# Strassen's scheme for the output projection of layer 0, with its products grouped by form

## The chip, the cores and the metric

One core of a Trainium2 chip runs the whole kernel in one launch. The metric is device microseconds (us) of that core. TensorE (PE) multiplies, VectorE (DVE) and ScalarE (ACT) do the elementwise work, GpSimd (POOL) and SyncE (SP) mostly issue transfers; each engine works through its instructions in order.

## What is computed

A trunk of two residual layers over 528 positions (16 meta tokens and a sequence of 512), model width 2048. Cut to what matters here:

```python
for layer in range(DEPTH):                       # DEPTH = 2
    hn = rms_norm(h, norm_gain[layer])
    y = even_mixer(hn, ...) if layer % 2 == 0 else odd_mixer(hn, ...)
    h = h + y
# the end of even_mixer (layer 0):
return jnp.concatenate([a_out, b_out], axis=-1) @ w_out      # (528 x 2048) @ (2048 x 2048)
# the end of odd_mixer (layer 1):
return o @ w_out                                             # (512 x 2048) @ (2048 x 2048)
```

`a_out` (1024 channels) comes from a convolution branch, `b_out` (1024 channels) from eight sparse attention heads.

## The kernel before, in words

Everything lies transposed: channels on the 128 partitions, positions along the free dimension (T = 528, cut in two halves of HT = 264). A vector of 2048 channels is 16 tiles of 128x528. The weights lie in DRAM in stripes of 128 output channels; a stripe is two halves of 128x1024 fp32 (512 KB), each with eight 128x128 blocks for 1024 input channels.

Matrix products are made in three passes: weights and inputs are split into a high and a low part, and `products` (L170 to L178) issues hi by hi, hi by lo and lo by hi for each of 8 blocks, so 24 matmuls for one weight half and one half of the positions. `load_half` (L140 to L148) loads a weight half on SP's queue into one of 2 staging tiles `w32`, copies it to `wh` on ACT (L146) and subtracts for `wl` on DVE (L147); `wh` and `wl` have 3 buffers each. `stripe` (L150) uses one weight half for both halves of the positions: 2 x 2 x 24 = 96 matmuls a stripe. `split` (L187 to L192) does the same splitting for an input tile.

Layer 0 runs in the order of the list `EVEN`: convolution (`glu`), index scores (`scores`), top-k selection (`select`), eight heads (`head`, with `attend`), then eight gate stripes that finish the tiles `MA[0..7]` of `a_out` (L608 to L620). `attend` writes each head's result to DRAM (`mbd`, L561). In `attend`, for each block of 128 queries, POOL issues a transfer of the bias rows (L516), then one that adds the mask in flight (L518); DVE takes both up at L526. The tiles `L` that they fill have 3 buffers.

**The stage that is changed** (L624 to L659): the eight `mbd` tiles are loaded and split, then the eight `MA` tiles; then 16 stripes, each with the `mbd` half first (`order=(1, 0)`). For each output tile the residual input is loaded on SP's queue (L645), DVE adds the two PSUM parts (L649), the sum is split for layer 1 (L190, L191), written to DRAM as `h1d` on SP's queue (L651), and squared and accumulated for the next norm (L656, L657).

**Layer 1** runs 16 recurrent heads, each with three stripes, while POOL's queue makes sums of weight halves in DRAM (`weight_sums`, L861 to L878: copies, and additions in flight). Then come 16 gate stripes, and then its own output projection, which already uses Strassen's scheme: the 2x2 blocks of weights and inputs give 7 products in place of 8, 56 products of 24 matmuls of 256 columns, each with a weight half of its own; every third load has a third staging tile, `w33`.

The order on each engine is set at build time by a scheduler that simulates the kernel; `band(level)` gives a stretch of code its priority (`WGT` 5 for weights, `EVAC` 4, `SIDE` 3, `CONV` 2). Among what is ready by that simulation, the higher band goes first.

Of the kernel before, what the change touches and what calls it, by code (L numbers as in the profile page):

```python
# [18 lines left out]
SEQ = 512  # L19
# [53 lines left out]
def trunk_kernel(ctx: ExitStack, tc: tile.TileContext, x: bass.AP, w: bass.AP, wukv: bass.AP,  # L73
# [42 lines left out]
    ones_c = ones_of(1.0 / 256, "ones_c")  # L116
    ones_a = ones_of(1.0 / 1024, "ones_a")
    ones_h = cst([128, 128], F32R, "ones_h")
    S.activation(ones_h, ones_c, AF.Copy, scale=2.0)
# [3 lines left out]
    V.memset(c15, 1.5)  # L123
    eps_l = cst([128, 1], F32, "eps_l")
# [3 lines left out]
    for _ in range(10):  # L128
        P.matmul(warm[:, :128], ones_d, ones_a, start=True, stop=True)
# [9 lines left out]

    def load_half(src, pool=wpool, names=("wh", "wl"), bufs=3, m=128, w32=None):  # L140
        w32 = w32 or wpool.tile([128, 1024], F32, name="w32", bufs=2)
        Q.dma_start(w32, src)
# [27 lines left out]
    def products(o, hi, lo, X, start, stop, m=128):  # L170

        issued = []
        for k, (xh, xl) in enumerate(X):
# [3 lines left out]
            issued.append(P.matmul(o, lo[:, ws], xh, start=False, stop=stop and k == 7))  # L177
        return issued  # L178

    def evac(dst, parts, rstd):  # L180
        o = T - dst.shape[-1]
        for p, sl in parts:
            V.tensor_tensor(dst[:, sl.start - o:sl.stop - o], p[:dst.shape[0]], rstd[:dst.shape[0], sl],  # L183
                            op=OP.mult)

# [20 lines left out]
    def rstd_from(pieces, dst, eps, tmp=None):  # L206

        for p, sl in pieces:
            S.activation(dst[:, sl], p, AF.Ln, bias=eps)
            S.activation(dst[:, sl], dst[:, sl], AF.Exp, scale=-0.5)  # L210
            if tmp is not None:
                t = tmp[:, sl]
                S.activation(t, dst[:, sl], AF.Square)
                V.scalar_tensor_tensor(t, p, eps, t, op0=OP.add, op1=OP.mult)
                S.activation(t, t, AF.Identity, scale=-0.5, bias=c15)
                V.tensor_tensor(dst[:, sl], dst[:, sl], t, op=OP.mult)

# [5 lines left out]
    r1 = tc.tile_pool(name="r1", bufs=KT, side="left")  # L223
    r1p = r1.__enter__()
    ev = ExitStack()
    epools = {}
# [4 lines left out]
    for role in ("em", "es", "ec", "ek", "ei"):  # L231
        epools[role] = ev.enter_context(tc.tile_pool(name=role, bufs=2, side="right"))
# [152 lines left out]
    with band(SIDE):  # L385
        rc = et([128, T], F32, "acc", 2)
        rstd_from(mean_bcast(ones_c, csq, None), rc, eps_r, et([128, T], F32, "sq", 3))
# [47 lines left out]
    def scores(j):  # L435
        ps = stripe(S_QI + j, X0, wide=False)

# [38 lines left out]
    def glu(i):  # L476
        ps = stripe(S_GLU + 2 * i, X0)
        g = et([128, T], F32, "gt", 3)
# [3 lines left out]
        ps = stripe(S_GLU + 2 * i + 1, X0)  # L482
        v = et([128, T], F32, "gt", 3)
# [94 lines left out]
    def layer_norm():  # L578
        with band(CONV):
# [5 lines left out]
            for p, sl in mean_bcast(ones_a, [zs], None):  # L585
                S.activation(mu[:, sl], p, AF.Copy)
# [10 lines left out]
            rstd_from(mean_bcast(ones_a, [vs_], None), rz, eps_l)  # L597
# [307 lines left out]

# [274 lines left out]
```

## Time and profile before

| | |
|---|---|
| median of 3 runs | 1944.06 us (1943.9 to 1944.37) |
| the profiled execution | 1945.34 us |
| its span, first to last instruction | 1943.1 us |
| mean granted TensorE clock | 0.997 of full |
| HBM read, written | 223.12 MB, 44.78 MB |
| PE / DVE / ACT / POOL busy | 99% / 70% / 44% / 6% |

Busy shares are over the whole span. A matmul's duration in the profile covers its way through the array, and the next one starts long before it ends; the time from one start to the next tells more than the duration. DVE and ACT instructions overlap a little as well. The idle time of an engine stands beside the instruction that followed it, with what ended it. The time of the runs contains some 2 us around the span.

### The profile page before, as it was taken

Reading aid. Unit: us, or ns where it says so; the run is one execution under the profiler, and the core shown is the slowest. Engines: PE = TensorE matmul, PEld = TensorE weight load, DVE = VectorE, ACT = ScalarE, POOL = GpSimd, SP = SyncE. Lnnn points to the kernel's source line nnn. Section 1 sums busy time; section 2 is a strip of 40 time slices with the busy share of each in tenths; the row PEclk is TensorE's granted clock in tenths of the full one; section 3 lists DMA queues with packets and bytes.
Section 4 is the critical chain, followed back from the end, with each engine's and each line's share of the span. In section 5 each row is a group of like instructions: output and inputs, shape, how many; then the busy total and the mean of one; then the engine's idle time right before and its main releaser. Section 6 shows DMA issues by size and latency. Waiting matters only on the chain.

```text
span 1943.1 us, 36429 instructions
## 1 busy us (share of the span) xinstructions
PE 1922.4 (99%) x14998; PEld 1813.8 (93%) x14998; DVE 1357.0 (70%) x2581; ACT 846.7 (44%) x1475; POOL 119.4 (6%) x202
## 2 busy tenths in 40 slices
PE   9999999999999999999999999999999999999997
PEld 8999899999999999999999999999999988889997
DVE  7699989997466444443677777777777775558766
ACT  6332442234435433322554545454555443235554
POOL 1000000111110100000000000000000000000000
PEclk9999999999999999999999999999999999999998
DMA  6323333344342434444644453444445423226665
GB/s 211 106 87 93 102 89 105 92 120 117 105 116 83 122 127 132 136 135 141 158 120 120 131 145 117 131 120 120 140 115 149 120 77 109 92 93 215 187 185 174
DMA packets 77302, 244.59 MB, mean 126 GB/s; under 512 B 9744, under 2 KB 17464, under 8 KB 76624
## 3 DMA queue, kind: packets, MB, share of 16 engines
q1 hardware_dynamic: 62656, 194.21, 30.8%
q0 software_dynamic: 14192, 47.86, 11.2%
q8 instruction: 118, 1.93, 0.4%
q14 instruction: 48, 0.39, 0.1%
q10 hardware_dynamic: 288, 0.19, 0.0%
HBM read 223.12 MB, written 44.78 MB: 138 GB/s over the span
## 4 chain that ended last, share of the span: by engine, by line
PE 80%; DVE 1%; DMA 0%; ACT 0%; issue 0%; DVEq 0%
PE mps L177 22%; PE mps L175 22%; PE mps L176 22%; PE s L176 1%; PE s L177 1%; PE s L175 1%; PE po L549 1%; PE s L524 1%; PE s L718 1%; PE s L717 1%; PE s L719 1%; PE po L840 1%; PE po L839 1%; PE s L836 1%; PE s L420 1%; PE s L407 0%
## 5 line engine op out<-in xcount | busy, mean ns | idle before, releaser
L175 PE MATMUL mps<-xh,wh 128*128 128x264 f32 (+2 forms) x3504 | 1074.2, 307 | 5.1 <-ACT xh L190 2.4
L177 PE MATMUL mps<-xh,wl 128*128 128x264 f32 (+2 forms) x3504 | 1075.1, 307 | 0.0
L176 PE MATMUL mps<-xl,wh 128*128 128x264 f32 (+2 forms) x3504 | 1073.7, 307 | 0.1
L175 PEld LDWEIGHTS mps<-xh,wh 128*128 128x128 f32 x3504 | 660.6, 189 | 34.9 <-ACT xh L190 2.6
L176 PEld LDWEIGHTS mps<-xl,wh 128*128 128x128 f32 x3504 | 659.5, 188 | 30.5 <-issue 0.6
L177 PEld LDWEIGHTS mps<-xh,wl 128*128 128x128 f32 x3504 | 659.7, 188 | 27.3
L146 ACT ACTIVATE wh<-w 128x1024 fp32r<-128x1024 f32 x313 | 331.5, 1059 | 595.1 <-PE mps L176 487.8
L147 DVE TENSOR_TENSOR wl<-w,wh 128x1024 fp32r<-128x1024 f32 x313 | 382.9, 1223 | 200.5 <-ACT wh L146 194.9
L494 DVE SCALAR_TENSOR_TENSOR z<-u,vec,z 128x528 f32<-128x528 f32 x240 | 180.6, 763 | 2.6
L183 DVE TENSOR_TENSOR gt<-mps,rstd 128x264 f32<-128x264 f32 (+1 forms) x80 | 38.5, 482 | 74.5 <-PE mps L177 73.5
L713 ACT ACTIVATE qhm<-q 128x256 f16<-128x256 f32 x128 | 51.8, 417 | 56.4 <-DVE q L815 44.3
L176 PE MATMUL s<-xl,wh 128*128 128x256 f32 (+1 forms) x240 | 67.7, 282 | 0.0
L175 PE MATMUL s<-xh,wh 128*128 128x256 f32 (+1 forms) x240 | 67.5, 281 | 0.0
L177 PE MATMUL s<-xh,wl 128*128 128x256 f32 (+1 forms) x240 | 67.4, 281 | 0.0
L800 DVE COPY_PREDICATED A<-msk,s 128x256 f32<-128x256 uint8 x96 | 46.5, 485 | 28.4 <-PE s L719 27.8
L714 DVE SCALAR_TENSOR_TENSOR qlm<-q,qhm 128x256 f16<-128x256 f32 x128 | 53.0, 424 | 15.8 <-ACT qhm L713 15.7
L649 DVE TENSOR_TENSOR hin<-mps,hin 128x264 f32<-128x264 f32 x32 | 13.8, 433 | 46.4 <-PE mps L177 46.4
L459 ACT ACTIVATE sq<-s 128x264 f32<-128x264 f32 (+3 forms) x80 | 29.2, 393 | 39.0 <-PE s L457 32.3
L713 ACT ACTIVATE kt1h<-k 128x256 f16<-128x256 f32 x64 | 26.5, 414 | 44.5 <-DVE k L806 44.5
L176 PEld LDWEIGHTS s<-xl,wh 128*128 128x128 f32 x240 | 45.1, 188 | 0.6 <-issue 0.6
L175 PEld LDWEIGHTS s<-xh,wh 128*128 128x128 f32 x240 | 45.2, 188 | 0.0
L177 PEld LDWEIGHTS s<-xh,wl 128*128 128x128 f32 x240 | 45.2, 188 | 0.0
(366 smaller groups left out, 2521.3 us busy)
## 6 DMA issues: line engine op xcount, KB each, us to landing
w<-in_w_dram SPq DMA_DIRECT2D x283, 512.0 KB, 3.7
ws<-in_w_dram POOLq DMA_DIRECT2D x48, 512.0 KB, 6.0
w<-ws SPq DMA_DIRECT2D x32, 512.0 KB, 3.6
ws<-ws POOLq DMA_DIRECT2D x16, 512.0 KB, 5.0
hin<-in_x_dram SPq DMA_DIRECT2D x16, 264.0 KB, 3.7
h1d<-hin SPq DMA_DIRECT2D x16, 264.0 KB, 2.1
on<-h1d SPq DMA_DIRECT2D x14, 256.0 KB, 4.2
z<-in_x_dram SPq DMA_DIRECT2D x8, 264.0 KB, 5.3
```

Source lines behind the costliest of these rows:

```text
L146: S.activation(uh, used, AF.Copy)
L147: V.tensor_tensor(ul, used, uh.bitcast(F32), op=OP.subtract)
L175: P.matmul(o, hi[:, ws], xh, start=start and k == 0, stop=False)
L176: P.matmul(o, hi[:, ws], xl, start=False, stop=False)
L177: issued.append(P.matmul(o, lo[:, ws], xh, start=False, stop=stop and k == 7))
L183: V.tensor_tensor(dst[:, sl.start - o:sl.stop - o], p[:dst.shape[0]], rstd[:dst.shape[0], sl], op=OP.mult)
L420: P.matmul(p[:ns, :256], CX[k][b][:, s0:s0 + ns], a[:, ws], start=n == 0, stop=n == 5)
L459: S.activation(r[:, :s1 - s0], p[:, :s1 - s0], AF.Relu)
L494: eng.scalar_tensor_tensor(z, u[:, j:j + T], col(V_CW + i * CW + j), z, op0=OP.mult, op1=OP.add)
L713: S.activation(hi, src, AF.Copy, scale=scale)
L714: V.scalar_tensor_tensor(lo, src, scale, hi, op0=OP.mult, op1=OP.subtract)
L800: V.copy_predicated(A.rearrange("p b (n a m) -> p b n a m", a=2, m=mm)[:, :, :, 1, :], msk[:, li - 1 + i:li + i, :].rearrange("p b (n m) - ...
```

## The change

The output projection of layer 0 is made of 7 products per pair of output tiles (output tiles p and p+8, for p from 0 to 7), over the two halves of positions and the two halves of input channels. All first products of the eight pairs run, then all of the next form: order 1, 5, 6, 7, 4, 3, 2.

- Weight sums for layer 0 (8 pairs, 8 transfers each, 512 KB each) are made in DRAM during layer 0: 16 plain copies on SP's queue behind weight loads of `scores` and `glu`, 48 copies and additions on POOL's queue behind the mask additions of the softmax. Those of layer 1 go on as before, 4 per recurrent head.
- The seven input forms: B11, N1 and N2 are split into a new pool `xf` in the place of three pools of layer 0; N2 reads `mbd` and writes an intermediate `tfd` to DRAM; T3, T4 (from `tfd`), B22 and B21 (from `mbd`) are loaded again on POOL's queue and split into the tiles `xh`, `xl` of layer 0's input.
- The residual inputs and outputs `C[0..15]` are held in tiles of layer 0 that are done with. Their loads and the writes of `h1d` move from SP's queue to POOL's.
- Layer 1's input `X1` goes into the tiles `xh`, `xl` again, rather than into a pool of its own. The first stripe of layer 1 and its last gate stripe take their halves in the order (1, 0).
- The first three products run seven of their eight blocks each, and the eighth blocks afterwards.
- The third staging tile is used for products 9, 12, 15, ... of both Strassen stages. In layer 1 it was used for every third from the third on.
- Three constants for means become one, with the factor moved into ACT's scale.

```diff
-        P.matmul(warm[:, :128], ones_d, ones_a, start=True, stop=True)
+        P.matmul(warm[:, :128], ones_d, ones_d, start=True, stop=True)
...
+    def sum_step(what, m, pair):
+        a = {11: w[pair[0], 0], 12: w[pair[0], 1], 21: w[pair[1], 0], 22: w[pair[1], 1]}
+        if what == "copy":
+            dst = wsum[pair, m] = dram.tile([128, 1024], F32, name=f"ws{pair[0]}_{m}")
+            src = {7: a[11], 5: a[21], 6: wsum.get((pair, 5)), 3: wsum.get((pair, 6))}[m]
+            return (Q if m in (5, 7) and pair in EPAIRS else G).dma_start(dst, src)
+        src = {7: a[21], 5: a[22], 6: a[11], 3: a[12]}[m]
+        return G.dma_start(wsum[pair, m], src, accum_op=OP.add, max_dma_last_dim=4096)
...
+    def strassen_weights(pair, m, pool, at):
+        own = at > 6 and at % 3 == 0
+        return load_half(product_weights(pair, m),
+                         w32=pool.tile([128, 1024], F32, name="w33", bufs=1) if own else None)
...
     def glu(i):
         ps = stripe(S_GLU + 2 * i, X0)
+        some_steps(plain_steps, 1, loaded[0])
...
-                G.dma_start(e[:, :W], M[t], accum_op=OP.add)
+                masked = G.dma_start(e[:, :W], M[t], accum_op=OP.add)
+                some_steps(steps, 1 + t % 2, masked)
...
-    for n in range(KT):
-        with band(EVAC):
-            hin = U.tile([128, T], F32, name="hin1", bufs=2)
-            Q.dma_start(hin, x[n])
-        ps = stripe(S_OE + n, MX, order=(1, 0))
...
     with band(SIDE):
+        for z in MA:
+            early_form0("B11", z[:, LT])
+        for z in MA:
+            n1 = et([128, T], F32, "sq", 3)[:, LT]
+            V.tensor_tensor(n1, z[:, LT], z[:, RT], op=OP.subtract)
+            early_form0("N1", n1)
+        for i, z in enumerate(MA):
+            mb = et([128, T], F32, "sq", 3)
+            G.dma_start(mb, mbd[i])
+            V.scalar_tensor_tensor(mb[:, RT], mb[:, RT], 2.0, z[:, RT], op0=OP.mult, op1=OP.subtract)
+            V.scalar_tensor_tensor(z[:, LT], mb[:, RT], -1.0, z[:, LT], op0=OP.mult, op1=OP.subtract)
+            V.scalar_tensor_tensor(mb[:, LT], mb[:, LT], -2.0, z[:, LT], op0=OP.mult, op1=OP.subtract)
+            G.dma_start(tfd[i], mb)
+            early_form0("N2", z[:, LT])
+        for name, src, sl, scale in (("T3", tfd, RT, 0.25), ("T4", tfd, LT, 0.25), ("B22", mbd, RT, 0.5),
+                                     ("B21", mbd, LT, 0.5)):
+            for j in range(0, 8, 2):
+                both = et([128, T], F32, "sq", 3)
+                G.dma_start(both.rearrange("p (n t) -> p n t", n=2), src[j:j + 2, :, sl].rearrange("n p t -> p n t"))
+                hl = split(r1p, both, scale)
+                forms0[name] += [[t[:, c] for t in hl] for c in (LT, RT)]
...
+    def finish1(n):
+        X1[n] = split(r1p, C[n], col(V_G1 + n))
+        G.dma_start(h1d[n], C[n])
...
+    turns = [(p, m) for m in (1, 5, 6, 7, 4, 3, 2) for p in range(8)]
+    for at, (pr, m) in enumerate(turns):
+        u, c0, c1 = us[pr], C[pr], C[8 + pr]
+        o = (mps if at % 7 < 3 else ps1)()[:, :HT]
+        with band(WGT):
+            hi, lo = strassen_weights(EPAIRS[pr], m, xfp, at)
+        X = forms0[FORM[m]]
+        if at < 3:
+            products(o, hi, lo, X[:7], True, False)
+            held.append((o, hi[:, 896:], lo[:, 896:]))
+            if at < 2:
+                continue
+            for o, hi, lo in held:
+                products(o, hi, lo, X[7:], False, True)
+        else:
+            products(o, hi, lo, X, True, True)
+        with band(EVAC):
+            if m == 1:
...
+                    S.activation(us[p], o, AF.Copy)
+                    V.tensor_tensor(C[p][:, LT], C[p][:, LT], o, op=OP.add)
+            elif m == 5:
+                V.tensor_tensor(c0[:, RT], c0[:, RT], o, op=OP.add)
+                V.tensor_tensor(c1[:, RT], c1[:, RT], o, op=OP.subtract)
+            elif m == 6:
+                V.tensor_tensor(u, u, o, op=OP.add)
+                V.tensor_tensor(c0[:, RT], c0[:, RT], u, op=OP.add)
+            elif m == 7:
+                V.tensor_tensor(u, u, o, op=OP.add)
+                both = c1.rearrange("p (c t) -> p c t", c=2)
+                V.tensor_tensor(both, both, u[:, None, :].to_broadcast([128, 2, HT]), op=OP.subtract)
+            elif m == 4:
+                V.tensor_tensor(c1[:, LT], c1[:, LT], o, op=OP.subtract)
+                finish1(8 + pr)
+            elif m == 3:
+                V.tensor_tensor(c0[:, RT], c0[:, RT], o, op=OP.add)
...
+                V.tensor_tensor(c0[:, LT], c0[:, LT], o, op=OP.add)
+                last = finish1(pr)
...
-        ps = stripe(S_FQV + 3 * h, X1)
+        ps = stripe(S_FQV + 3 * h, X1, order=(0, 1) if h else (1, 0))
...
-        weight_sums(h // 2, h % 2, cleared)
+        some_steps(osteps, 4, cleared)
```

## Rows read from the trace of the kernel before

**Rows 1.** The page's parts 1 and 2: busy time, the span in 40 slices.

```profile
PE 1922.4 (99%) x14998; PEld 1813.8 (93%) x14998; DVE 1357.0 (70%) x2581; ACT 846.7 (44%) x1475; POOL 119.4 (6%) x202
...
PE   9999999999999999999999999999999999999997
```

**Rows 2.** Evacuations of the changed stage, DVE's timeline: start, us, instruction, idle before.

```profile
762.42 0.43 DVE L649 TENSOR_TENSOR hin<-mps,hin 128x264 f32<-128x264 f32 x1 [0.70 <-PE mps L177]
...
914.96 0.43 DVE L649 TENSOR_TENSOR hin<-mps,hin 128x264 f32<-128x264 f32 x1 [0.70 <-PE mps L177]
917.88 0.43 DVE L649 TENSOR_TENSOR hin<-mps,hin 128x264 f32<-128x264 f32 x1 [2.49 <-PE mps L177]
```

**Rows 3.** The end of the last gate stripe, DVE's timeline.

```profile
727.19 0.43 DVE L183 TENSOR_TENSOR gt<-mps,rstd 128x264 f32<-128x264 f32 x1 [1.20 <-PE mps L177]
...
731.16 0.70 DVE L619 TENSOR_TENSOR z<-z,gb 128x528 f32<-128x528 f32 x1
```

**Rows 4.** The changed stage's first stripe, PE's timeline.

```profile
733.47 0.28 PE L177 MATMUL mps<-xh,wl 128*128 128x264 f32 x1
736.11 0.63 PE L175 MATMUL mps<-xh,wh 128*128 128x264 f32 x3 [2.36 <-ACT xh L190]
```

**Rows 5.** Windows: us, busy time by engine, PEclk, DMA share, GB/s.

```profile
core 0: us, PE busy (x) PEld busy (x) DVE busy (x) ACT busy (x) POOL busy (x), PEclk, DMA share, GB/s
698.00:727.00 29.00, 29.00 (x239) 29.00 (x239) 15.48 (x22) 9.67 (x14) 0.00 (x0) 1.00 0.43 137
727.00:745.00 18.00, 15.53 (x126) 15.11 (x125) 11.76 (x18) 9.18 (x16) 0.00 (x0) 1.00 0.27 81
745.00:915.00 170.00, 170.00 (x1394) 170.00 (x1392) 68.31 (x90) 49.17 (x60) 0.95 (x1) 1.00 0.42 139
1790.00:1920.00 130.00, 130.00 (x1097) 130.00 (x1096) 92.28 (x136) 72.56 (x104) 0.00 (x0) 1.00 0.60 186
925.00:960.00 35.00, 35.00 (x282) 32.81 (x281) 24.97 (x56) 18.34 (x38) 4.52 (x7) 1.00 0.74 181
0.00:20.00 20.00, 17.96 (x117) 15.93 (x118) 14.23 (x33) 15.75 (x27) 3.84 (x16) 1.00 0.94 333
```

**Rows 6.** Groups of instructions of the changed stage (745 to 915 us).

```profile
L147 DVE TENSOR_TENSOR wl<-w,wh 128x1024 fp32r<-128x1024 f32 x30 | 36.8, 1225 | 59.1 <-ACT wh L146 59.1
L146 ACT ACTIVATE wh<-w 128x1024 fp32r<-128x1024 f32 x30 | 31.7, 1058 | 121.9 <-PE mps L176 71.1 <-issue 50.7
...
L191 DVE SCALAR_TENSOR_TENSOR xl<-hin,vec,xh 128x528 fp32r<-128x528 f32 x15 | 11.5, 763 | 0.0
L190 ACT ACTIVATE xh<-hin,vec 128x528 fp32r<-128x528 f32 x15 | 10.8, 720 | 0.0
L657 DVE TENSOR_TENSOR acc<-acc,sq 128x528 f32<-128x528 f32 x14 | 9.8, 702 | 0.0
```

**Rows 7.** A split of 256 columns, and eight back to back (DVE).

```profile
L919 DVE TENSOR_TENSOR xl<-on,xh 128x256 fp32r<-128x256 f32 x32 | 11.6, 419 | 0.0
...
737.37 5.03 DVE L191 SCALAR_TENSOR_TENSOR xl<-z,xh 128x528 fp32r<-128x528 f32 x8
```

**Rows 8.** Weight splits in layer 1's Strassen stage: first and last start.

```profile
L146 ACT ACTIVATE wh<-w x46: 1058/1062/1062, 1789.6 to 1917.5; 128x1024 fp32r<-128x1024 f32 x46
```

**Rows 9.** Transfers, median us from issue to landing: 745 to 915, then 925 to 960.

```profile
w<-in_w_dram SPq DMA_DIRECT2D x30, 512.0 KB, 3.7
...
w<-in_w_dram SPq DMA_DIRECT2D x6, 512.0 KB, 4.2
ws<-in_w_dram POOLq DMA_DIRECT2D x4, 512.0 KB, 7.4
```

**Rows 10.** A head's last query block: mask transfer issued, DVE's use; then all mask transfers.

```profile
638.91 0.87 POOL L518 DMA_DIRECT2D L<-mask  x1 [4.32 <-PE s L546]
...
645.91 0.42 DVE L526 CUSTOM_DVE_ANT_0 L<-s,L 128x264 f32<-128x264 f32 x1
...
DMA to landing us min/median/max: 2.4/3.5/5.8
```

**Rows 11.** Two of the eight lines of weight sums in layer 1, on POOL's queue.

```profile
L871 POOL DMA_DIRECT2D ws<-in_w_dram x8: 514/516/517, 921.1 to 1488.8; - x8
L872 POOL DMA_DIRECT2D ws<-in_w_dram x8: 838/844/849, 925.4 to 1493.8; - x8
```

More of the change, by code (lines that the diff above doesn't have):

```diff
@@ L176, in products @@
             P.matmul(o, hi[:, ws], xl, start=False, stop=False)
-            issued.append(P.matmul(o, lo[:, ws], xh, start=False, stop=stop and k == 7))
+            issued.append(P.matmul(o, lo[:, ws], xh, start=False, stop=stop and k == len(X) - 1))
         return issued
@@ L221, in trunk_kernel @@
     h1d = dram.tile([KT, 128, T], F32, name="h1d")
[L223 to L226, printed above, removed]
+    tfd = dram.tile([8, 128, T], F32, name="tfd")
+    r1p = ctx.enter_context(tc.tile_pool(name="r1", bufs=KT, side="left", reuse_waits="tile"))
+    epools, eopen = {}, {}
     def et(shape, dt, name, bufs):
         return epools[EROLE.get(name, "es")].tile(shape, dt, name=name, bufs=bufs)
-    for role in ("em", "es", "ec", "ek", "ei"):
-        epools[role] = ev.enter_context(tc.tile_pool(name=role, bufs=2, side="right"))
+    for role in ("em", "ec", "es", "ek", "ei"):
+        eopen[role] = tc.tile_pool(name=role, bufs=2, side="right")
+        epools[role] = eopen[role].__enter__()
     E = epools["ek"]
@@ L622, in trunk_kernel @@
         tap("ma7", MA[7])
-    MX = [None] * KT
-    with band(SIDE):
-        for i in range(8):
-            mb = et([128, T], F32, "mb", 2)
-            Q.dma_start(mb, mbd[i])
-            MX[8 + i] = split(r1p, mb, 0.5)
-        for i in range(8):
-            MX[i] = split(r1p, MA[i], 0.25)
-    ev.close()
-    r2 = tc.tile_pool(name="r2", bufs=KT, side="right", reuse_waits="tile")
-    r2p = r2.__enter__()
-    up = tc.tile_pool(name="up", bufs=2, side="right", reuse_waits="tile")
-    U = up.__enter__()
@@ L639, in trunk_kernel @@
[L639 to L659 removed]
+    for role in ("ei", "ek", "es"):
+        eopen[role].__exit__(None, None, None)
@@ new lines, in trunk_kernel, with early_form0 @@
+    keep = ctx.enter_context(tc.tile_pool(name="keep", bufs=1, side="left", reuse_waits="tile"))
+    xf = tc.tile_pool(name="xf", bufs=1, side="right", reuse_waits="tile")
+    xfp = xf.__enter__()
+    LT, RT = slice(0, HT), slice(HT, T)
+    forms0 = {name: [] for name in FORM.values()}
+    def early_form0(name, src):
+        hi, lo = [xfp.tile([128, HT], F32R, name=n, bufs=24) for n in ("fh", "fl")]
+        split2(hi, lo, src, 0.25)
+        forms0[name].append((hi, lo))
+    with band(SIDE):
+        for z in MA:
[19 more added lines that the diff above has]
+                forms0[name] += [[t[:, c] for t in hl] for c in (LT, RT)]
@@ L928, in late_form @@
         if i % 2 == 0:
-            late[name] = [r2p.tile([128, T], F32R, name=n, bufs=KT) for n in ("xh", "xl")]
+            late[name] = [r1p.tile([128, T], F32R, name=n, bufs=KT) for n in ("xh", "xl")]
         sl = slice(i % 2 * HS, (i % 2 + 1) * HS)
@@ L976, in trunk_kernel @@
                 late_form(name, i)
[L979 to L986 removed]
     pending = []
     H2 = [None] * KT
[L989 removed]
+    acc2 = keep.tile([128, T], F32, name="rstd1", bufs=1)[:, :SEQ]
     done = [0, 0]
```

135 lines of the change are left out of this document (73 added, 62 removed).

## The prediction

> **What bounds the kernel now.** I read the page's busy times first, then the windows of the changed stage, then the starts of its evacuations, its waits and its transfers. PE is busy in 1922.4 of 1943.1 us and in nearly every slice [rows 1]: a microsecond leaves the time only if PE has fewer matmuls or fewer gaps. In the stage itself PE is busy in 170.0 of 170 us at full granted clock, DVE in 68.3, ACT in 49.2, POOL in 0.95, and the transfers move 139 GB/s [rows 5]. So the stage lasts as long as its matmuls take to issue. The first evacuation of a stripe comes at 762.42 us, that of the stripe 13 further on at 914.96 [rows 2]: 11.734 us a stripe, 122.2 ns a matmul (96 of them), 2.933 us for the 24 of one product.
>
> **What is removed.** 16 stripes are 64 groups of 24 matmuls; Strassen's scheme leaves 56. Eight groups by 2.933 us are **23.5 us**. The second term is a wait: between the last evacuations of the gate stripes (727.19) and of the stage (917.88) [rows 2, 3] lie 190.7 us, and 16 stripes by 11.734 are 187.7, so some **2.9 us** are lost. They are where PE stood from 733.47 to 736.11 for the split of a late `mbd` tile [rows 4]. The new order doesn't need `mbd` until the third group of products, so this wait goes.
>
> The Trainium skill (TensorE: Matmul & The Clock Gate, section Back-to-back issue gap) gives N/2.4 + 2.5 ns for an isolated gap, 112.5 ns for 264 columns; by it the first term would be 21.6 us. The measured 122.2 ns decides.
>
> **What is added, in the order of the stage.** First the start. B11 needs `MA[7]`, whose last product ends some 4.7 us after the last gate evacuation (731.16 + 0.70 against 727.19) [rows 3], and after that come a copy on ACT and a subtraction on DVE of 264 columns, about 0.4 us each as in the 256-column row [rows 7]. The three products of seven blocks cover 63 matmuls, 7.7 us, so no wait here. But they keep all three pairs of weight buffers until their eighth blocks have run. Only then can the fourth product's weights be split: 1.06 us on ACT, then 1.22 on DVE [rows 6], about 0.2 for the handovers, against six held matmuls (0.7) and two that need no `wl` (0.2): **1.6 us** of wait.
>
> Then the staging tiles. Until product 9 there are only two, and a product now uses up a weight half in 2.933 us where a stripe took 5.87. A staging tile is taken for the landing (3.7 us, 4.2 beside POOL's sums [rows 9]) and the split (2.3): 6.0 to 6.5 us for two products that take 5.87. With the cushion of ready weights used up by the held blocks, I count waits of a few tenths at products 5 and 7 by the 3.7, and about 1 us each by the 4.2. Bounds 0.7 and 4 us (the 7.4 that a landing on POOL's queue took [rows 9] would be the worst case for one or two of them); I take **2 us**, as the stage's start is where its extra loads crowd. From product 9 on three tiles serve three products in 8.8 us, enough up to a landing of about 6 us. Layer 1 has this steady state now: 46 splits from 1789.6 to 1917.5, 2.84 us each [rows 8], with PE busy throughout [rows 5]. Its own third tile now comes in later; there the buffers start full, which I cost at nothing, between nothing and 1 us.
>
> **DVE** gets close to its limit. Per stage: 56 weight subtractions (1.225) 68.6 us; 72 evacuating operations of 264 columns (0.433, [rows 2]) and 8 of 528 (0.70) 36.8; 16 finished tiles (0.763 and 0.702 [rows 6]) 23.4; forms, 56 operations of 264 (0.42 [rows 7]) and 16 of 528 (0.70) 34.7. Together 163.5 us of busy time in 56 x 2.933 = 164.3. Three things relieve it. Instructions back to back overlap: eight of 0.70 took 5.03 us, not 5.6 [rows 7], which is a tenth of it all. The forms of `MA[0..6]` can be made in the 29 us before the stage, where DVE is busy in 15.5 [rows 5]. And weights come first in priority, while seven PSUM buffers let an evacuation be up to six products late. What is left is a load of 80 to 90%, against the 71% (92.3 of 130) that layer 1's stage bears without a wait [rows 5]. Bounds 0 and 8 us (the overdue work of the second group, two evacuations a product plus what remains of N2); I take **2 us** together with what follows.
>
> **Queues and transfers.** SP loses 40 transfers of 264 KB and gets 16 copies behind weight loads in layer 0, where a weight half lasts over 5 us: nothing, 0 to 1 us. POOL, idle in the stage, issues 64 transfers there at 0.5 to 0.85 us [rows 11]. What waits in that queue: a load of `mbd` stands behind a write of `tfd` whose tile it needs, and the loads of `C[8..15]` behind N2. With three such tiles the eight rounds of N2 take some 25 us; due is the last one 47 us after the start, T3's at 70 us. The transfers of the stage are 56 weight halves (29.4 MB), residuals in and out (8.7 MB), `mbd` and `tfd` (8.7 MB): 46.7 MB in 164 us, 285 GB/s. The trace has 186 GB/s at a share of 0.60 and 333 at 0.94 [rows 5], so this is high but below what was reached.
>
> At the **handover** to layer 1, X1[4..7] overwrite the B21 tiles and are split only after the last product: four times 0.72 and 0.763 [rows 6] with a weight split between them, about 5 us. The first stripe begins with the other half, 48 matmuls, 5.9 us. Nothing, 0 to 1 us.
>
> In the **attention**, 48 sums join POOL's queue, 0.5 to 0.85 us each [rows 11]. What is behind them is the next block's bias transfer. The mask of a head's last block is issued at 638.91 and used at 645.91; it takes 0.87 us and 3.5 to land, so about 2.6 us are spare, in the tightest head [rows 10]. One or two sums and a slower landing take about that. I cost it at nothing, 0 to 5 us.
>
> **Sum**, on the profiled execution's 1945.34 us: -23.5 - 2.9 + 1.6 + 2 + 2 = -20.8, so 1924.5. The median of the runs lies 1.3 us below that execution: **1923 us**. No change, as far as a measurement tells, is within 0.2%, 3.9 us.
>
> **Rivals.**
> *Transfers hold the stage.* If the crowded start (loads of C, `mbd`, `tfd`, all beside the weights) or the 285 GB/s can't be kept up, weights land late again and again. At 260 GB/s, halfway between the two rows, 46.7 MB take 180 us, 16 more: 1937. For it: weights landed in 4.2 us rather than 3.7 beside only four sums [rows 9]. Against it: 333 GB/s in the first 20 us [rows 5]. The Trainium skill (DMA: Bandwidth & Descriptors, section Issuing engines are not separate DMA queues) says that transfers from any queue share the same 16 engines and interleave; by that rule moving them to POOL's queue spares the weights nothing, and the two landings in [rows 9] agree. Chance 0.14, 1930 to 1940.
>
> *Slower than before: the masks.* The sums' transfers run beside the softmax's bias and mask transfers. If a mask lands later than the spare 2.6 to 5 us, DVE waits at L526 with the weight subtractions queued behind it, and PE follows once the ready weights are used. There are 8 such last blocks. To cancel the gain, each must lose over 2.6 us, that is a mask 7 us late or more; at 12 us, each loses about 7 and the time is 1923 + 56 = 1979; at 8 us, 1923 + 28 = 1951. For it: a sum took 7.4 us to land [rows 9]. Against it: the mask is 3.5 us at the median and 5.8 at most [rows 10], and the other blocks' masks are issued far ahead. Chance 0.07.
>
> *It doesn't shorten the stage.* If weights arrive at no better than one per 3.35 us, 56 of them take as long as before: 1944. It would take a landing of over 7 us on three tiles. Chance 0.04; layer 1's 2.84 us speaks against it.
>
> *Nothing new waits* but the fourth product: 1944.06 - 26.4 + 1.6 = 1919. The chance of 1917 to 1920 is 0.10.
>
> **The numbers.** My own case, waits of 3 to 10 us in all, 1920 to 1930, has 0.65. With the other cases: faster by over 0.2% 0.88, the same 0.05, slower 0.07. The range 1917 to 1937 holds the better case, my own and most of the first rival.
>
> **What would show it.** Right: 192 matmuls fewer; last gate evacuation to last product of the stage about 170 us, not 190.7; a wait of PE for `wh` or `wl` at the fourth product; DVE busy in over 80% of the stage; weights landing in 4 to 5 us there; attention without new waits of PE. Wrong: PE waits for weights spread over all seven groups (transfers), waits of DVE for DMA at L526 (masks), or at N2 and T3 (forms late).

## The result, and the profile after

The changed kernel takes **1923.73 us** (median of 4 runs, 1923.7 to 1924.42) where the kernel before takes 1943.98 on the same chip (1943.82 to 1944.37): a ratio of 0.9896, 95% interval 0.9879 to 0.9914. The profiled execution took 1923.71 us, its span is 1921.9. Other chips of the study gave the kernel before 1944.8 to 1945.3 and the changed one 1925.72, so times below are set against runs on the same chip.

The page's busy times of the changed kernel, the answer to [rows 1]:

```profile
PE 1897.4 (99%) x14806; PEld 1790.5 (93%) x14806; DVE 1421.1 (74%) x2708; ACT 883.5 (46%) x1531; POOL 193.6 (10%) x314
```

There are 192 matmuls fewer, and PE is still busy nearly all the time. To see where the microseconds went, the span is cut at three places in PE's timeline: the first product of layer 0's output stage, the first matmul of layer 1, and the first product of layer 1's output stage.

| us | until layer 0's output | layer 0's output | layer 1's heads and gates | layer 1's output to the end | span |
|---|---|---|---|---|---|
| before | 726.98 | 190.69 | 850.68 | 174.71 | 1943.1 |
| after | 728.51 | 167.97 | 848.51 | 176.94 | 1921.9 |
| difference | +1.5 | -22.7 | -2.2 | +2.2 | -21.2 |

At the 2.933 us of the kernel before, 56 products take 164.3 us, which leaves 3.7 us of delay. But where no wait falls, this stage's matmuls start a little closer: 121.67 ns apart (1137 starts in a row from 758.01 to 896.36 us) in place of 122.2. That makes 2.920 us a product and 163.5 us for 56, so the delay is 4.4 us. Windows of the changed kernel over the stage (columns as in [rows 5]); the last row is all of it:

```profile
728.72:752.00 23.28, 21.52 (x171) 20.66 (x169) 19.62 (x40) 12.56 (x25) 5.38 (x10) 1.00 0.70 232
752.00:775.00 23.00, 22.01 (x176) 21.57 (x177) 18.57 (x36) 10.41 (x14) 7.06 (x14) 1.00 0.91 312
775.00:799.00 24.00, 24.00 (x199) 24.00 (x198) 22.36 (x40) 13.40 (x16) 7.55 (x12) 1.00 0.94 345
...
728.72:897.60 168.88, 166.13 (x1354) 164.84 (x1353) 142.96 (x227) 95.12 (x129) 33.53 (x57) 1.00 0.77 263
```

DVE, in 68.31 of 170 us before [rows 5], is now busy in 142.96 of 168.88, 85%. The transfers rose from a share of 0.42 to 0.77, with 0.91 and 0.94 between 752 and 799 us. PE isn't busy throughout in the first two windows only. These are all its waits in the stage, and some matmuls beside the first two (PE's timeline; the wait stands in brackets):

```profile
737.15 0.29 PE L179 MATMUL mps<-fh,wl 128*128 128x264 f32 x1
737.78 0.39 PE L177 MATMUL s<-fh,wh 128*128 128x264 f32 x1 [0.34 <-ACT wh L148]
738.01 0.28 PE L178 MATMUL s<-fl,wh 128*128 128x264 f32 x1
739.00 0.39 PE L177 MATMUL s<-fh,wh 128*128 128x264 f32 x1 [0.71 <-ACT wh L148]
739.23 0.28 PE L178 MATMUL s<-fl,wh 128*128 128x264 f32 x1
...
748.39 0.39 PE L179 MATMUL s<-fh,wl 128*128 128x264 f32 x1 [0.37 <-DVE wl L149]
751.93 0.39 PE L179 MATMUL mps<-fh,wl 128*128 128x264 f32 x1 [0.34 <-DVE wl L149]
755.42 0.39 PE L177 MATMUL mps<-fh,wh 128*128 128x264 f32 x1 [0.55 <-ACT wh L148]
756.37 0.39 PE L177 MATMUL mps<-fh,wh 128*128 128x264 f32 x1 [0.44 <-ACT wh L148]
```

The first two are the products behind the three held ones, the fourth and the fifth: 1.05 us. The other four, 1.70, are weights that came late: ACT stood ready for them (ACT's timeline), since they hadn't landed.

```profile
742.45 1.06 ACT L148 ACTIVATE wh<-w 128x1024 fp32r<-128x1024 f32 x1 [2.31 <-DMA w<-in_w_dram]
...
754.31 2.01 ACT L148 ACTIVATE wh<-w 128x1024 fp32r<-128x1024 f32 x2 [3.33 <-DMA w<-ws]
```

A wait costs more than its bracket, which counts only the idle time after the end of the matmul before. From 737.15 to 737.78 are 0.63 us and from there to 738.01 are 0.23, where 0.12 each is the rule: 0.62 us for a bracket of 0.34. So it is with all six, some 0.28 us more each: 1.6 us at the fourth and fifth products and 2.8 for the late weights, which is the 4.4 us of delay.

Over the whole stage the median landing is 4.6 and 3.8 us, against 3.7 before [rows 9] (transfers issued from 728 to 897 us):

```profile
w<-ws SPq DMA_DIRECT2D x31, 512.0 KB, 4.6
w<-in_w_dram SPq DMA_DIRECT2D x24, 512.0 KB, 3.8
```

Layer 1's output stage, up to its final norm, has no wait in the kernel before but one of 0.44, and three now (PE's timeline), 2.56 us:

```profile
1757.35 0.38 PE L177 MATMUL s<-eh,wh 128*128 128x256 f32 x1 [1.24 <-ACT wh L148]
1758.61 0.39 PE L179 MATMUL s<-eh,wl 128*128 128x256 f32 x1 [0.56 <-DVE wl L149]
1768.69 0.39 PE L179 MATMUL mps<-xh,wl 128*128 128x256 f32 x1 [0.76 <-DVE wl L149]
```

Ahead of layer 0's output PE waits 6.97 us in all where it waited 5.04: three times for a softmax tile (0.58, 0.51 and 0.77 us) in place of once (0.60), and once more for a buffer of the evacuations (0.53).

### The profile page after: what moved, and what is told of

The parts are those of the page before. It is cut to its first block, busy times and chain, and to the rows that moved or that the text cites. A ratio compares the mean times of both kernels' runs of the same rounds, so it can differ in the third digit from the quotient of the medians.

```text
span 1921.9 us, 36451 instructions
## 1 busy us (share of the span) xinstructions
PE 1897.4 (99%) x14806; PEld 1790.5 (93%) x14806; DVE 1421.1 (74%) x2708; ACT 883.5 (46%) x1531; POOL 193.6 (10%) x314
## 4 chain that ended last, share of the span: by engine, by line
PE 87%; issue 5%; DMA 3%; DVE 3%; POOL 1%; ACT 1%; SPq 0%; DVEq 0%; POOLq 0%; ACTq 0%
PE mps L177 23%; PE mps L179 23%; PE mps L178 22%; PE s L177 3%; PE s L178 3%; PE s L179 3%; PE po L614 1%; DMA L<-bdram 1%; DMA w<-ws 1%; PE s L863 1%; PE s L862 1%; PE s L864 1%; PE po L985 1%; PE po L984 1%; PE s L589 1%
## 5 line engine op out<-in xcount | busy, mean ns | idle before, releaser
L177 PE MATMUL mps<-xh,wh 128*128 128x264 f32 (+2 forms) x3088 | 956.8, 310 | 2.8 <-DVE gt L185 2.8
L179 PE MATMUL mps<-xh,wl 128*128 128x264 f32 (+2 forms) x3088 | 956.2, 310 | 0.8 <-DVE wl L149 0.8
L178 PE MATMUL mps<-xl,wh 128*128 128x264 f32 (+2 forms) x3088 | 953.6, 309 | 0.0
L177 PEld LDWEIGHTS mps<-xh,wh 128*128 128x128 f32 x3088 | 582.3, 189 | 31.0 <-DVE gt L185 2.9
L178 PEld LDWEIGHTS mps<-xl,wh 128*128 128x128 f32 x3088 | 581.3, 188 | 29.4 <-issue 0.6
L179 PEld LDWEIGHTS mps<-xh,wl 128*128 128x128 f32 x3088 | 581.6, 188 | 28.4 <-DVE wl L149 1.0
L177 PE MATMUL s<-xh,wh 128*128 128x256 f32 (+1 forms) x400 | 113.4, 284 | 0.0
L179 PE MATMUL s<-xh,wl 128*128 128x256 f32 (+1 forms) x400 | 113.1, 283 | 0.0
L178 PE MATMUL s<-xl,wh 128*128 128x256 f32 (+1 forms) x400 | 113.0, 283 | 0.0
L249 POOL DMA_DIRECT2D ws<-in_w_dram x64 | 61.8, 1045 | 108.8 <-DMA ws<-ws 70.1
```

Of the source, the lines that this page charges most:

```text
L177: P.matmul(o, hi[:, ws], xh, start=start and k == 0, stop=False)
L178: P.matmul(o, hi[:, ws], xl, start=False, stop=False)
L249: return G.dma_start(wsum[pair, m], src, accum_op=OP.add, max_dma_last_dim=4096)
```

## The experiments

My theory after the result: the stage is bound by its matmuls, the delays at its start come from too little buffering and crowded transfers; layer 1's +2.2 us are the later third staging tile; the +1.5 us ahead of the stage are the weight sums beside the softmax. The rivals: the transfers' rate is the bound of the stage, or DVE; the sums cost nothing.

How far a single profile can be trusted shows where the code is the same. Up to the first product of the stage, seven profiles of the same code (the changed kernel's two and five of kernels that differ from it only later) take 727.72 to 730.93 us. The stage itself takes 167.97, 168.61, 169.10, 169.23 and 169.85 us in the five that leave it and its buffers as they are and do not add transfers. So a difference of under 2 us in one of these stretches shows little by itself. Layer 1's output is steadier: 176.36 to 177.55 us in nine profiles with the later third tile.

### The wait that went: late `mbd` tiles alone

The kernel before, with five tiles in place of two for the loads of `mbd`.

```diff
-            mb = et([128, T], F32, "mb", 2)
+            mb = et([128, T], F32, *(("mb", 2) if i % 5 < 2 else ("L", 3)))
```

> The kernel before, with five tiles instead of two for loading the head results that its output projection starts with (three of them in the place of the softmax's tiles). My theory: the 2.9 us that its first stripe loses wait for a load that has no tile yet, so with five they go: about 1941 to 1941.8 beside 1944.0 of the kernel before. Rival: the load is late because of its place in SP's queue or of the input tiles that the split overwrites, and nothing changes: 1943.8 to 1945.

Measured: 1942.5 us beside 1945.07, a span of 1940.3 where it was 1943.1. PE's wait of 2.36 us [rows 4] is gone and no other took its place; the stage takes 187.73 us where it took 190.69. So this wait was worth 2.6 to 3.0 us, as priced, and that could have been had without the rest of the change.

### The price of a product group

The matmuls of product 3 are issued twice for each of the eight pairs.

```diff
+            if m == 3:
+                products(o, hi, lo, X, True, True)
             products(o, hi, lo, X, True, True)
```

> The eight products of the sixth group (B22) of layer 0 are issued twice into the same PSUM tile, the second time starting afresh: 192 matmuls more, nothing else. My theory: the stage is bound by PE there, and each product of 24 matmuls costs 2.93 us: +23.5, 1947. Rival: weights or VectorE set the pace of that group, and the second pass hides in it: +10 to +20.

Measured: 1951.31 us; the stage takes 194.77, so 26.8 more. Eight groups by the 2.920 us of this kernel are 23.4 of them. PE's waits in the stage come to 4.37 us where they were 2.75, 1.6 more, and the granted clock fell once, behind a wait of 1.43 us (PE's timeline):

```profile
757.30 0.39 PE L177 MATMUL mps<-fh,wh 128*128 128x264 f32 x1 [1.43 <-ACT wh L148]
...
758.85 0.42 PE L179 MATMUL mps<-fh,wl 128*128 128x264 f32 x1
759.07 0.42 PE L177 MATMUL mps<-fh,wh 128*128 128x264 f32 x1
...
761.99 0.28 PE L177 MATMUL mps<-fh,wh 128*128 128x264 f32 x1
762.11 0.29 PE L178 MATMUL mps<-fl,wh 128*128 128x264 f32 x1
```

Matmuls start 220 ns apart and, from 761.5 us on, 122 ns again. The windows from 756 to 760 and from 760 to 764 us have granted clocks of 0.76 and 0.81: 4 x 0.24 + 4 x 0.19 = 1.7 us lost by the shares. By the starts it is 1.4 us, since a matmul at the low level takes 220 ns in place of 122, not twice the time. 23.4 + 1.6 + 1.4 is the 26.8 but for 0.4. The term of the sum holds, and the stage's matmuls are on the path to the end one for one.

### Which buffer delays the start of the stage

Two kernels: the third staging tile for products 2, 5, 8, ... in both Strassen stages, and two products held rather than three.

```diff
-        own = at > 6 and at % 3 == 0
+        own = at % 3 == 2
```

> The third staging tile from the third product on, in both Strassen stages (loads 2, 5, 8, ... instead of 9, 12, 15, ...). My theory: after the held products, the changed kernel's waits of PE for weights (0.37 + 0.34 + 0.55 + 0.44 us at products 5 to 8 of layer 0; 1.24 + 0.56 + 0.76 us at the start of layer 1's stage) come from having two staging tiles only, with landings of 5.5 to 5.9 us. They should mostly go: 1923.7 becomes 1919.5 to 1921. Rival: the transfers as such are too slow there (an 85 to 95 percent busy share), so an earlier issue lands no earlier: 1923 to 1924. A second rival, slower by 1 to 3 us: the tile's place is still in use when the load wants it.

```diff
-        if at < 3:
+        if at < 2:
...
-            if at < 2:
+            if at < 1:
```

> Two products instead of three run seven blocks first. My theory: the two still cover the split of the last B11 tile (two times 21 matmuls, 5.1 us, against 4.7 us from the first product to that split's end in the changed kernel's trace), and the third pair of weight buffers stays free, so the wait for the fourth product's weights (0.34 + 0.71 us, and what follows from late staging) goes: 1922 to 1923. Rival: the cover is too short and PE waits for the last tile instead, up to 1 us: 1923.5 to 1925.

Measured, third tile: 1921.65 us (1918.45 to 1924.86) beside 1945.3, a ratio of 0.9878, 0.9864 to 0.9893. Its profile took 1920.4 us, 3.3 less than that of the changed kernel on another chip, and 3.06 of that is layer 1's stage (173.88 us in place of 176.94). Layer 0's stage is no shorter: 167.98 us. The four waits for late weights at 748 to 756 us went, so those did come from having two staging tiles. Two others came (PE's timeline, and what stood before them on DVE and ACT):

```profile
780.48 0.39 PE L178 MATMUL mps<-fl,wh 128*128 128x264 f32 x1 [0.84 <-DVE fl L195]
...
820.44 0.39 PE L179 MATMUL mps<-xh,wl 128*128 128x264 f32 x1 [1.31 <-DVE wl L149]
```

```profile
778.17 0.43 DVE L788 TENSOR_TENSOR z<-z,s 128x264 f32<-128x264 f32 x1 [1.33 <-DMA z<-in_x_dram]
...
816.91 0.65 ACT L201 ACTIVATE xh<-sq 128x528 fp32r<-128x528 f32 x1 [2.91 <-DMA sq<-mbd]
817.46 1.05 ACT L148 ACTIVATE wh<-w 128x1024 fp32r<-128x1024 f32 x1
```

The first is for a form of N2: DVE had stood 1.33 us for the load of a residual, with the form's split behind it. The second is for a weight: ACT had stood 2.91 us for a load of `mbd` for the form B21, which only the last group of products needs, and took the weight's copy up directly behind it. Both loads are on POOL's queue. So what held PE next were loads on that queue that DVE and ACT take up in order, not weights that landed late.

Two products held: 1923.48 us (1923.34 to 1924.99), 0.989, 0.9873 to 0.9906; the stage takes 168.26. The wait of 0.34 us at the fourth product is gone (by the starts, the delay there is 1.25 us in place of 1.6), and the late weights cost more (3.5 in place of 2.8). Neither edit shortens the stage by what a single profile can tell. In all three kernels the transfers run in its first 70 us at shares of 0.91 to 0.97 (with the earlier third tile 0.97 and 0.95, with two held 0.94 twice). That alone doesn't hold PE: with the earlier third tile it is busy in 23.00 of 23 us from 752 to 775, at 0.97.

### Is it the transfers

28 copies of 512 KB from DRAM to DRAM, on SP's queue behind the weight loads of the stage.

```diff
             hi, lo = strassen_weights(EPAIRS[pr], m, xfp, at)
+            if at % 2:
+                with tc.issue_after(loaded[0].ins):
+                    Q.dma_start(spare[at // 2], w[S_FQV + at, 0])
```

> The changed kernel with 28 more copies of 512 KB within DRAM on SP's queue, one behind every second weight load of layer 0's output stage (14.7 MB more; nothing reads them). It prices the rival that transfers hold the stage. My theory: at 263 GB/s and a busy share of 0.77 over the stage there is room for some of it, but the first three groups already run at 0.91 to 0.94; the 59 MB would need 352 GB/s to fit in 168 us, more than any window shows (345), so weights land late and the stage grows by 5 to 15 us: 1929 to 1939. Rival: there is room throughout, within 1 us of 1923.7.

Measured: 1933.84 us, the stage 174.92, 7.0 more. The share over the whole stage is 0.91, up from 0.77, and PE waits for weights as late as 862 us, 7.35 us in all where it was 2.75. Windows of this kernel at the same places (columns as above):

```profile
755.00:778.00 23.00, 20.20 (x155) 19.25 (x156) 16.54 (x32) 8.39 (x12) 6.02 (x12) 1.00 0.96 345
778.00:802.00 24.00, 22.58 (x185) 22.37 (x184) 18.98 (x33) 10.41 (x13) 5.77 (x9) 1.00 0.96 367
802.00:825.00 23.00, 23.00 (x191) 23.00 (x191) 20.98 (x32) 13.21 (x16) 5.69 (x8) 1.00 0.97 359
```

At a share of 0.96, PE loses 2.8 and 1.4 us in the first two windows; at 0.97 in the third it loses nothing. The rest of the stage, at 0.62 to 0.78 in the changed kernel, bore its copies with waits of 1.24 us. So a third more bytes cost 5 to 7 us, set against the stage of the same code, most of them in the first 70 us, but the share by itself doesn't say whether PE waits. The copies also stand on SP's queue in front of later weight loads; this run doesn't tell that from the rate. That the transfers as such bind the changed kernel at its start isn't shown: no run with fewer transfers in that stretch was made, and with one staging tile more the weights came in time.

### The weight sums beside the softmax

Without the 48 sums on POOL's queue in layer 0 (products 3, 5, 6 and 7 take plain weight halves of the same size instead, so this kernel computes something else), and with 48 copies of 512 KB more behind the same masks.

```diff
...
-             for pr in EPAIRS[g:g + 4]]
+             for pr in EPAIRS[g:g + 4]][:0]
```

> Leaves out the 48 weight sums of layer 0 on POOL's queue; products 3, 5, 6, 7 of layer 0 take plain weight halves of the same size from the input instead, so that part of the computation is changed. My theory: the 1.5 us by which layer 0 up to the last gate stripe got longer are waits for the softmax behind these transfers, so the last gate evacuation comes at 727.2 again, not 728.7, and the time is 1921.5 to 1922.7. Rival: the 1.5 us are an accident of the changed order of instructions and stay: 1923.7.

```diff
                 some_steps(steps, 1 + t % 2, masked)
+                with tc.issue_after(masked.ins):
+                    for _ in range(1 + t % 2):
+                        G.dma_start(spare[spare_at[0]], w[S_OE + spare_at[0] % 16, 0])
+                        spare_at[0] += 1
```

> The changed kernel with 48 more copies of 512 KB on POOL's queue, as many behind each mask addition of the softmax as the weight sums (nothing reads them). It prices the rival on the slower side. The 48 sums themselves cost 2.0 us of layer 0 (first product at 728.5 with them, 726.5 without). My theory: the spare time of the last blocks' masks is then used up, so the cost grows faster than the count but stays a matter of a few waits: first product 3 to 8 us later, 1927 to 1932. Rival: each of the 8 last blocks is held by several us: 20 us or more later, 1944 or above.

Measured without them: 1921.49 us, the stage begins at 726.49, 2.0 us sooner than at 728.51; PE waits 5.17 us up to there, nearly as little as in the kernel before. The seven profiles with the sums lie 1.2 to 4.4 us above it, so the sums cost something, and 2.0 us is a size from one pair of them. With 48 more: 1955.73 us, and the stage begins at 758.07, 29.6 later. My theory had 1927 to 1932 there and was wrong; the rival had it. PE waits six times for a softmax tile, 19.7 us in all. Three of them (PE's timeline), and windows around the same places with their granted clock:

```profile
509.57 0.66 PE L613 MATMUL s<-ident,L 128*128 128x128 f32 x4 [3.51 <-ACT L L604]
...
559.29 1.12 PE L613 MATMUL s<-ident,L 128*128 128x128 f32 x4 [5.11 <-ACT L L604]
...
717.06 1.11 PE L613 MATMUL s<-ident,L 128*128 128x128 f32 x4 [3.67 <-ACT L L604]
```

```profile
508.00:516.00 8.00, 6.43 (x41) 6.23 (x42) 2.21 (x7) 3.46 (x9) 0.00 (x0) 0.79 0.98 308
557.00:569.00 12.00, 9.71 (x57) 9.20 (x58) 3.81 (x9) 4.76 (x11) 3.00 (x5) 0.72 0.83 220
714.00:726.00 12.00, 8.94 (x53) 8.40 (x54) 6.44 (x15) 4.92 (x11) 0.59 (x1) 0.72 0.90 275
```

The waits are 17.8 us more than the changed kernel's 1.9, and behind them the clock is low: 8 x 0.21 + 12 x 0.28 + 12 x 0.28 is 8.4 us by the shares in these three windows, and with 0.57 from 497 to 501 and 0.66 from 592 to 597, behind two more of the waits, 11.8. That is too much by two things. In some 2.3 us of the low time PE stood idle, and the shares put half of it down as lost, 1.2 us. And they take half of the rest as lost, where a matmul that starts 220 ns after the last in place of 122 loses 98 of 220, 0.89 of a half. So an estimate of what the clock cost is (11.8 - 1.2) x 0.89 = 9.4 us, and together with the waits that is 27.2 of the 29.6. The bias rows that each block needs first land later and later (transfers from 300 to 720 us of this kernel; the same row read 3.3 us in the kernel before and 6.6 in the changed one, both from 300 to 700):

```profile
spare<-in_w_dram POOLq DMA_DIRECT2D x47, 512.0 KB, 9.0
...
L<-bdram POOLq DMA_DIRECT2D x7, 264.0 KB, 8.3
```

This is the prediction's slower rival, the masks, with one step different: the masks of 264 KB land in 3.5 us here and in 3.8 in the kernel before, so it is the bias rows ahead of them that come late. The change as made stands some 2 us into it, and with 48 transfers more it is slower than the kernel before.

### Forms tile by tile

B11, N1 and N2 of each tile one after the other, rather than each form for all eight tiles.

```diff
-        for z in MA:
-            early_form0("B11", z[:, LT])
-        for z in MA:
+        for i, z in enumerate(MA):
+            early_form0("B11", z[:, LT])
...
-        for i, z in enumerate(MA):
             mb = et([128, T], F32, "sq", 3)
```

> The changed kernel with the forms B11, N1 and N2 made tile by tile (all three of tile 0, then of tile 1, ...) instead of form by form. In the changed kernel's trace all splits of N1 and all of N2 stand behind the split of the last B11 tile, so the loads and stores of N2 crowd into the first 45 us of the stage. My theory: most of this work moves into the 30 us before the stage, where VectorE is busy in half of the time; the weights then land sooner and 1.5 to 3 us of PE's 2.75 us of waits after the third product go: 1920.5 to 1922. Rival: the tiles' places come free too late, or N2's loads hold VectorE in the gate stripes: 1923.5 to 1926.

Measured: 1927.45 us, the stage 170.40: 2.4 more than in the changed kernel's profile, though only 0.5 more than in the longest of the same code. There is no gain, and the trace shows a new wait. N2 of an earlier tile waits for its `mbd` load, and the last step of `MA[7]` (L684) stands behind it on DVE, and with it the eighth block of the first products (DVE's timeline, then PE's):

```profile
736.85 0.43 DVE L713 SCALAR_TENSOR_TENSOR sq<-sq,z 128x264 f32<-128x264 f32 x1 [1.48 <-DMA sq<-mbd]
737.20 0.70 DVE L684 TENSOR_TENSOR z<-z,gb 128x528 f32<-128x528 f32 x1
```

```profile
739.07 0.64 PE L177 MATMUL mps<-fh,wh 128*128 128x264 f32 x3 [1.78 <-ACT fh L194]
```

In the changed kernel L684 runs at 731.56. PE's waits in the stage are three now and come to 2.77 us, as much as the six of the changed kernel (2.75). What the stage is longer by is the clock's: behind the 1.78 us it is 0.59 and 0.73 from 740 to 750 us. By the shares that is 5 x 0.41 + 5 x 0.27 = 3.4 us, but PE stood idle in 0.8 us of the low time; by the starts 2.5 us are lost.

### The third tile in layer 1 alone, and sums made earlier

On one chip: the changed kernel again, put at 1923.7 us within 1 and measured 2 above; the third tile for products 2, 5, 8, ... in layer 1's stage alone; 16 of the 48 sums moved ahead of the heads, so that each mask has one sum behind it; and both edits.

> The changed kernel itself, beside the three kernels that follow. 1923.7 as before, within 1.

```diff
-            hi, lo = strassen_weights(OPAIRS[pr], m, fp, at)
+            hi, lo = strassen_weights(OPAIRS[pr], m, fp, at, at % 3 == 2)
```

> Only layer 1's output projection gets its third staging tile for products 2, 5, 8, ... again, layer 0's keeps it from product 9 on. My theory: the 2.2 us that layer 1's stage takes longer than in the kernel before come from the later third tile alone, so all of the gain of third_tile is there: first layer-1 output product to the end 173.9 us rather than 176.9, the stage of layer 0 168.0 as now, the time 1920.9 (about 2.5 to 3 us below after_again). Rival: third_tile's spread of 1918.5 to 1924.9 hides that there is no gain: within 1 us of after_again.

```diff
+    early_steps = steps[:16]
+    del steps[:16]
...
         some_steps(plain_steps, 1, loaded[0])
+        if len(plain_steps) < 8:
+            some_steps(early_steps, 2, loaded[0])
...
-                some_steps(steps, 1 + t % 2, masked)
+                some_steps(steps, 1, masked)
```

> 16 of the 48 weight sums on POOL's queue go behind weight loads of the index scores and convolution (two per stripe, from the ninth stripe on), and the other 32 one behind each softmax mask, where one or two stand now. My theory: what the sums cost are late masks and bias rows in the attention (leaving all 48 out brought the first product of the stage 2.0 us forward, 48 more pushed it back by 29.6), and this cost grows steeply with their number per block, so most of the 2 us comes back: first product at 726.5 to 727.5, the time 1922 to 1923. Rival: the early transfers make the stripes' weights late, as the stripes run with two staging tiles: first product at 728.5 or later, 1924 to 1927.

> Both edits, early_sums and late_tile. They lie in stretches 1000 us apart, so their gains add: 4 to 5 us below after_again, 1919 to 1920. If early_sums goes its rival's way, 1921 to 1924.

| | median us | runs | first product of the stage | layer 1's output to the end |
|---|---|---|---|---|
| changed kernel again | 1925.72 | 1924.68 to 1925.89 | 729.13 | 177.22 |
| third tile in layer 1 | 1921.87 | 1920.69 to 1924.57 | 730.51 | 173.90 |
| sums earlier | 1942.51 | 1938.31 to 1948.83 | 745.12 | 176.94 |
| both | 1937.5 | 1934.42 to 1940.9 | 744.72 | 173.86 |

The third tile in layer 1 brings 3.3 us where it was due, and the median falls by 3.85. (In its profiled execution, the slowest of its runs, the softmax waits ahead of the stage took 2.6 us.) This and the third tile in both stages are the best versions found: ratios to the kernel before of 0.988 (0.9867 to 0.9893) and 0.9878.

The earlier sums were a plain miss, of theory and rival alike. The softmax waits are gone: from 380 to 720 us PE waits for no softmax tile, where the changed kernel on this chip has 1.1 us. But the additions, out from 37.67 us on, stand in POOL's queue until the transfers that they build on have landed, and small transfers stand among them. Behind one addition is a transfer of the index scores (POOL's timeline):

```profile
84.14 0.83 POOL L249 DMA_DIRECT2D ws<-in_w_dram  x1 [15.32 <-DMA ws<-in_w_dram]
...
97.27 0.81 POOL L249 DMA_DIRECT2D ws<-in_w_dram  x1 [0.62 <-DMA ws<-in_w_dram]
97.81 1.36 POOL L512 DMA_DIRECT2D uh<-ql  x2
```

The changed kernel issues this one at 90.16 us, and it lands in 2.6 us where it now takes 8.4. Most of the later issue isn't the queue's: the input `ql` is itself made at 96.49 us in place of 89.19, behind the first of the waits below. What PE waits for is the landing. PE's three waits for such transfers (all of PE's waits, by what they were for: us in total, times, longest):

```profile
PE s L443 <- DMA z<-in_onehot_dram: 4.0, 1, 4.0
PE s L522 <- DMA uh<-ql: 3.7, 1, 3.7
...
PE s L522 <- DMA ul<-ql: 1.9, 1, 1.9
```

These 9.6 us come with a granted clock of 0.83 from 60 to 80 and from 100 to 120 us and 0.96 from 120 to 160: 3.4 + 3.4 + 1.6 = 8.4 us by the shares. With some 1.4 us of it idle, the same estimate gives (8.4 - 0.7) x 0.89 = 6.9 us. Together 16.5, and the stage begins 16.0 later. With both edits the third tile's 3.1 us are there again: the gains add, but one of them was a loss.

## Why the prediction was right

The time, 1923 us, and the range held, and so did the case I thought likeliest. Its parts did less well: each of the four stretches is off, by 1.5 to 2.2 us, and the errors cancel. That the sum came within 1 us is luck; that the stage loses eight groups and the `mbd` wait, and gains a few short waits at its start, is not.

- **Eight groups, -23.5, and the `mbd` wait, -2.9.** Right: 192 matmuls fewer; eight more of the groups cost their 23.4 and what waits and the clock add; the wait alone is worth 2.6 to 3.0. Not in the sum: the other matmuls of the stage start 0.55 ns closer, 0.7 us.
- **The fourth product, +1.6.** Right, where it was said and for `wh`: brackets of 1.05 us, 1.6 by the starts. Part of it stands at the fifth product, whose first two matmuls the scheduler put in front of those of the fourth that need `wl`. Holding two products took a fifth of it, with no gain in the end.
- **Two staging tiles, +2, and DVE with the queues, +2.** The late weights cost 1.70 us in brackets and 2.8 by the starts, for the 4 that I put. On the second chip the same code took 169.10 and 169.85 us, 5.6 and 6.3 more than its matmuls' 163.5; I had 5.6 for all three terms of the start. The mechanism of the first held: with a third tile early these waits go. What I hadn't seen is that other waits then take their place, behind loads on POOL's queue. The landings that PE waited for were those of the crowded start that the first rival speaks of; from 757 us on the stage was free of them.
- **DVE over 80%.** 85%, without a wait that lasts. One thing that relieved it I had wrong: of the forms of `MA[0..6]` only B11 was split ahead of the stage. The scheduler put all splits of N1 behind the eighth B11, at 732.76 us (DVE's timeline):

```profile
732.76 0.43 DVE L195 SCALAR_TENSOR_TENSOR fl<-z,fh 128x264 fp32r<-128x264 f32 x1 [0.49 <-ACT fh L194]
733.11 0.77 DVE L195 SCALAR_TENSOR_TENSOR fl<-sq,fh 128x264 fp32r<-128x264 f32 x2
```

- **Transfers, 285 GB/s.** 263 over the stage; the peak, 345, is above the 333 that I had as reached.
- **The attention, 0 (0 to 5).** The step "One or two sums and a slower landing take about that. I cost it at nothing" failed: leaving the sums out gives some 2.0 us. I looked at the mask's landing, and the bias rows ahead of it, which start each block, are what slows most: 3.3 to 6.6 us.
- **Layer 1's third tile, 0 (0 to 1).** The step "there the buffers start full, which I cost at nothing" failed: +2.2 us for the stretch, and 3.0 to 3.3 come back with the tile. The full buffers last for nearly four products of 2.8 us (the first wait stands behind 93 matmuls); then two staging tiles serve it, up to the ninth, as at the start of layer 0's stage.
- **Layer 1's heads and gates, -2.2.** Not in the prediction. No wait is behind it: both kernels issue the same 6708 matmuls there, and those of 512 columns, 1535 of them in the stripes, start closer together. The gates show it, 643 matmuls in a row without a wait, the first and the last (PE's timeline, before and then after), 149.09 us and 148.38:

```profile
1619.03 0.40 PE L177 MATMUL mps<-xh,wl 128*128 128x512 f32 x1
...
1768.12 0.40 PE L177 MATMUL mps<-xh,wl 128*128 128x512 f32 x1
```

```profile
1596.38 0.40 PE L179 MATMUL mps<-xh,wl 128*128 128x512 f32 x1
...
1744.76 0.39 PE L179 MATMUL mps<-xh,wl 128*128 128x512 f32 x1
```

Over heads and gates these 1535 take 361.2 us before and 359.2 after, 2.1 of the 2.2. The stretch takes 850.68 us in both kernels of the old form and 848.51 in all twelve profiles of the new one, so it comes with the change and not with the execution. What in the change does it is open: the order of the first stripe's halves, the sums of layer 1 in another order, and the input in other tiles weren't tried one by one.

The chance of 0.07 for the masks looks low now: the price was paid in part, and 48 transfers more cost 29.6 us after the first 48 had cost some 2.

## What to carry to other kernels

Where the matmuls bind, count them, then look at every place where buffers or a queue start afresh: the eight groups came out to some tenths, and the waits were nearly all at such starts. Read what a wait cost from the starts, not from its bracket. A queue that has spare time can still not take more transfers in front of a small one that an engine waits for: price the landing and the order in the queue, not the issue time. And when a buffer is added and the wait only moves, look at what the new wait is for before adding another: here it was another queue's loads.

## What the hardware showed beyond that

A short wait of PE can cost more than itself. After 1.43 us (beside several short ones) matmuls started 220 ns apart in place of 122 for 3 us, after 1.78 us the granted clock was 0.59 and 0.73 in two windows of 5 us; the level that it falls to is 1.2 GHz, 0.5 of full. The wait of 2.36 us in the kernel before [rows 4] left the clock at 1.00 [rows 5]. At the start of layer 1's output stage, waits of 1.21 and 0.57 us in the kernel without the sums were followed by a clock of 0.72 from 1756 to 1762 us, and 1.24 and 0.56 in the changed kernel by 1.00 in the same window. So the length of the waits alone doesn't tell. Where waits came often, as with the added copies, the clock cost half as much as the waits by the estimate above.

The same matmuls, without a wait and at full clock, needn't start at the same distance: 264 columns took 122.2 and 121.7 ns in layer 0's output, 512 columns 232.2 and 231.1 in layer 1's gates, before and after. What decides it isn't shown.

The Trainium skill (DMA: Bandwidth & Descriptors, section Issuing engines are not separate DMA queues) has transfers of all queues interleave on the same engines. One run agrees: with additions on POOL's queue the weights on SP's land in 4.7 us in place of 3.5 (50 to 150 us, sums made earlier against the changed kernel on that chip).
